# Attention loads reordered in a hybrid decoder layer: running sums and boundary values behind the first chunk's keys and queries

## The chip, the cores and the metric

The kernel runs on one core of a Trainium2 chip. The metric is the device time of one execution in microseconds (us), as the median of several runs; the profile is taken from one more execution on the same core, whose own time and span are given below. Engines are named as the profile names them: PE is TensorE's matmul side, PEld its weight loads, DVE is VectorE, ACT is ScalarE, POOL is GpSimd, SP is SyncE, which here issues nearly all transfers.

## The reference

One decoder layer over 2048 tokens of width 1024, in float32. The normed input is multiplied by `w_in`, and its columns go to four mixers: stick-breaking attention (A, 4 heads of 64), spatial gating (B), RWKV-7 time mixing (C) and forgetting attention (D, 4 heads of 64). The four results are concatenated, multiplied by `w_out` and added to the input; a mixture of 32 experts and a last norm follow. The change touches only the loads of A and D:

```python
# A: stick-breaking attention, per block of 128 queries
z = einsum('bhqd,bhkd->bhqk', q, k) * scale
log_one_minus = where(strict, log_sigmoid(-z), 0)
between = cumsum(log_one_minus, reverse=True) - log_one_minus
out = where(strict, exp(log_sigmoid(z) + between), 0) @ v
# D: forgetting attention
cum = cumsum(log_f)                       # one running sum per head
logits = q @ k.T * scale + cum[q] - cum[k]
out = softmax(where(causal, logits, -inf)) @ v
```

## The kernel before

The work is laid out in stages: `in_proj` (products with `w_in`, written to the DRAM scratch arrays `sT`, channels by tokens, and `sV`, tokens by channels), `rwkv`, `attention`, the output projection, routing, the experts. `forget_gate` writes the running sums of D to `cumD`. The program text runs `rwkv` to its end before `attention` starts, but the order in which each engine meets its instructions is set by a planner (`schedule_with_timeline_sim=True`): when the kernel is built, it goes through a simulated time line and gives each engine, at each moment, the earliest instruction of the text that is ready. So instructions of RWKV and of attention stand mixed in every engine's queue, and so do the transfers in SP's queue. On the chip each queue is then run strictly in the order written.

`attention` goes through the 4 heads of A (`sb` is true), then the 4 of D, each in 8 blocks of 256 queries. A head's keys, queries and values come in 4 chunks of 512 tokens; `Head.load(c)` brings chunk c when the first block that needs it starts. It loads the key rows twice into the two halves of a tile `raw` (L341), makes the rounded part `kh` (L344, ACT in A) and the rest `kl` (L345, POOL), loads the query rows in the same way into the other of the two `raw` buffers (L348), and makes `qs` (L350 on ACT, then L351 on POOL). Then come the values `v` (L353) and, in A, the values shifted by one token, `u` (L358 to L361), from which POOL makes differences (L362). In D a chunk of running sums, `nk`, comes instead (L365).

A block of A is: logits on PE (`logits`, L375, L376 and, on the diagonal, L378), `tanh` on ACT (L390), an affine step on POOL (L391), a running product on DVE (L393), transposes (L425), copies (L427) and products with `v` (L431). At the end of a block the boundary values `vc` (the last value row of each block of 128 tokens) are added: in block 0 by a DVE copy (L444), otherwise in an ACT instruction (L442). `vc` is loaded when a head of A is created (L335): 64 by 16 single elements of 4 bytes.

`cq` holds the running sums of D by query, [128, 16, 4]. Four transfers (L321), one per head, fill it at the top of `attention`, each of 2048 single elements of 4 bytes. It is read in `softmax` alone, by L408 and L409, in heads of D.

L667 loads the inputs of RWKV, L673 is the DVE instruction that consumes them, L157 writes the last blocks of `in_proj`, and L1027 to L1030 (`route_setup`) write initial tables for the routing; in the text they stand inside head 0 of A, ahead of everything of head 1.

Of the kernel before, what the change touches and what calls it, by code (L numbers as in the profile page):

```python
# [8 lines left out]
F32 = mybir.dt.float32  # L9
# [11 lines left out]
NT = 16  # L21
W = 256
NH = 4
HD = 64
# [4 lines left out]
def dram(ap, offset, pattern):  # L29
    return bass.AP(tensor=ap.tensor, offset=ap.offset + offset, ap=pattern)  # L30
# [277 lines left out]
def attention(tc, K, ctx, sT, sV, cumD, mixT):  # L308
    nc = tc.nc
    cp = ctx.enter_context(tc.tile_pool(name="at_c", reuse_waits="tile", bufs=1))  # L310
    hp = ctx.enter_context(tc.tile_pool(name="at_h", reuse_waits="tile", bufs=5))
    rp = ctx.enter_context(tc.tile_pool(name="at_r", reuse_waits="tile", bufs=2))
# [3 lines left out]
    ps = ctx.enter_context(tc.tile_pool(name="at_ps", reuse_waits="tile", bufs=4, space=PSUM))  # L316
    po = ctx.enter_context(tc.tile_pool(name="at_po", reuse_waits="tile", bufs=1, space=PSUM))
    cq = cp.tile([128, NT, NH], F32, name="cq")
    with nc.allow_non_contiguous_dma(reason="small"):
        for h in range(NH):  # L320
            nc.sync.dma_start(cq[:, :, h], cumD[h].rearrange("(i p) -> p i", p=128))  # L321

    def bank():
        return ps.tile([128, 512], F32, name="bk", tag="bk")
# [1 line left out]
    class Head:  # L326
        def __init__(self, h, sb):
            self.h, self.sb = h, sb
            self.q0, self.k0, self.v0 = (0, 256, 0) if sb else (512, 768, 256)
            self.q0, self.k0, self.v0 = (a + h * HD for a in (self.q0, self.k0, self.v0))  # L330
            self.kh, self.kl, self.qs, self.v, self.nk = [], [], [], [], []
            if sb:
                self.vc = cp.tile([64, NT], F32, name="vc", bufs=2)
                with nc.allow_non_contiguous_dma(reason="small"):
                    nc.sync.dma_start(self.vc, dram(sV, 127 * 516 + self.v0, [[1, HD], [128 * 516, NT]]))  # L335

        def load(self, c):
            h, t0 = self.h, c * 512
            raw = rp.tile([128, 512], F32, name="raw", tag="raw")
            for s in range(2):  # L340
                nc.sync.dma_start(raw[s * 64:s * 64 + 64], sT[self.k0:self.k0 + HD, t0:t0 + 512])  # L341
            kh = hp.tile([128, 512], F32R, name="kh")
            kl = hp.tile([128, 512], F32R, name="kl")
            (nc.scalar.activation(kh, raw, AF.Copy) if self.sb else nc.gpsimd.tensor_scalar(kh, raw, 1.0, 0.0, op0=OP.mult, op1=OP.add))  # L344
            nc.gpsimd.tensor_sub(kl, raw, kh.bitcast(F32))  # L345
            raw = rp.tile([128, 512], F32, name="raw", tag="raw")
            for s in range(2):
                nc.sync.dma_start(raw[s * 64:s * 64 + 64], sT[self.q0:self.q0 + HD, t0:t0 + 512])  # L348
            qs = hp.tile([128, 512], F32R, name="qs", bufs=2)
            (nc.scalar.activation(qs, raw, AF.Copy) if self.sb else nc.gpsimd.tensor_scalar(qs, raw, 1.0, 0.0, op0=OP.mult, op1=OP.add))  # L350
            nc.gpsimd.tensor_sub(qs[64:128], raw[64:128], qs[64:128].bitcast(F32))  # L351
            v = hp.tile([128, 4, HD], F32, name="v")
            nc.sync.dma_start(v, sV[t0:t0 + 512, self.v0:self.v0 + HD].rearrange("(i p) c -> p i c", p=128))  # L353
            if self.sb:
                u = rp.tile([128, 4, HD], F32, name="u")
                if c == 0:
                    nc.vector.memset(u[0:1, 0], 0.0)
                    nc.sync.dma_start(u[1:128, 0], sV[0:127, self.v0:self.v0 + HD])  # L358
                    nc.sync.dma_start(u[:, 1:4], sV[127:511, self.v0:self.v0 + HD].rearrange("(i p) c -> p i c", p=128))
                else:  # L360
                    nc.sync.dma_start(u, sV[t0 - 1:t0 + 511, self.v0:self.v0 + HD].rearrange("(i p) c -> p i c", p=128))  # L361
                nc.gpsimd.tensor_sub(v, u, v)  # L362
            else:
                nk = hp.tile([128, 512], F32, name="nk", bufs=4)
                nc.sync.dma_start(nk, cumD[h:h + 1, t0:t0 + 512].to_broadcast([128, 512]))  # L365
                nc.gpsimd.tensor_scalar(nk, nk, -8.0, 0.0, op0=OP.mult, op1=OP.add)
                self.nk.append(nk)
            for l, t in ((self.kh, kh), (self.kl, kl), (self.qs, qs), (self.v, v)):
                l.append(t)
# [1436 lines left out]
def model(ctx, tc, x, xT, g1, w_in, wsT, bT, mu, w0, w2, a0, a2, g2, k_k, k_a, r_k, gn_w, gn_b, bf, w_out, g2b,  # L1806
# [15 lines left out]
    with tc.tile_pool(name="r_consts", bufs=1) as rp:  # L1822
        R = RwConsts(tc, K, rp)
        rw = rwkv(tc, K, R, right, sT, prm, mixT)
        in_proj(tc, K, x, xT, g1, w_in, wsT, bT, bf, sT, sV, mixT, cumD, lambda j: [next(rw) for _ in range((0, 1, 2, 0)[j])])
        with ExitStack() as left:
            init = left.enter_context(tc.tile_pool(name="init", bufs=1))
            for _ in rw:
                pass
            mix = attention(tc, K, left, sT, sV, cumD, mixT)  # L1830
            for _ in range(60):
                next(mix)
            route_setup(tc, init, table, gtab, xacc)
            for _ in mix:
                pass
# [58 lines left out]
```

## Time and profile before

| | |
|---|---|
| median of 3 runs | 2596.97 us (2595.97 to 2601.28) |
| the profiled execution's own time | 2600.24 us |
| its span, first to last instruction | 2598.5 us |
| mean granted TensorE clock | 0.968 |
| busy share of the span: PE, DVE, ACT, POOL | 94%, 65%, 51%, 26% |

The span is the stretch that the trace covers; the execution's own time is 1.7 us longer. Busy shares are means over stages with different limits, so the stages have to be read one at a time: `in_proj` with the first part of RWKV up to about 597 us, attention with the rest of RWKV from there to about 1525 us, the output projection and the experts after that.

### The profile page before, as it was taken

Reading aid. Unit: us, or ns where it says so; the run is one execution under the profiler, and the core shown is the slowest. Engines: PE = TensorE matmul, PEld = TensorE weight load, DVE = VectorE, ACT = ScalarE, POOL = GpSimd, SP = SyncE. Lnnn points to the kernel's source line nnn. Section 1 sums busy time; section 2 is a strip of 40 time slices with the busy share of each in tenths; the row PEclk is TensorE's granted clock in tenths of the full one; section 3 lists DMA queues with packets and bytes.
Section 4 is the critical chain, followed back from the end, with each engine's and each line's share of the span. In section 5 each row is a group of like instructions: output and inputs, shape, how many; then the busy total and the mean of one; then the engine's idle time right before and its main releaser. Section 6 shows DMA issues by size and latency. Waiting matters only on the chain. (4 is left out here: it accounts for less than half of the span.)

```text
span 2598.5 us, 42227 instructions
## 1 busy us (share of the span) xinstructions
PE 2444.1 (94%) x14802; PEld 1753.0 (67%) x14803; DVE 1679.6 (65%) x3881; ACT 1322.4 (51%) x2527; POOL 677.1 (26%) x691
## 2 busy tenths in 40 slices
PE   8999999997989899999999999997999999999994
PEld 6789998874646464656556668874666676676663
DVE  5313402247797879786685756665777787787785
ACT  6201222224665564575566642222666776777774
POOL 2000000016364646331331022222212232222224
PEclk9999999998989998999999999998999999999997
DMA  8510222215121111111101056744979899899995
GB/s 258 163 63 26 80 69 67 71 60 124 35 53 29 47 39 39 47 50 47 49 27 48 10 171 180 234 139 114 339 263 352 309 320 368 292 324 356 328 316 169
DMA packets 241826, 394.73 MB, mean 152 GB/s; under 512 B 65921, under 2 KB 106753, under 8 KB 241608
## 3 DMA queue, kind: packets, MB, share of 16 engines
q1 hardware_dynamic: 222472, 336.68, 39.2%
q0 software_dynamic: 19136, 55.30, 7.6%
q8 instruction: 118, 1.93, 0.3%
q14 instruction: 100, 0.82, 0.1%
HBM read 319.24 MB, written 76.85 MB: 152 GB/s over the span
## 5 line engine op out<-in xcount | busy, mean ns | idle before, releaser
L72 DVE TENSOR_TENSOR wl<-wr,wh 128x1024 fp32r<-128x1024 f32 x366 | 442.4, 1222 | 116.9 <-ACT wh L71 106.8
L71 ACT ACTIVATE wh<-wr 128x1024 fp32r<-128x1024 f32 x366 | 381.4, 1057 | 150.7 <-PE pg L1456 57.9
L393 DVE TENSOR_TENSOR_SCAN S<-S,zero 128x512 f32<-128x512 f32 (+3 forms) x160 | 198.5, 1251 | 48.8 <-POOL S L391 48.6
L152 PE MATMUL p<-hhi,wh 128*128 128x512 f32 x512 | 205.5, 403 | 11.6 <-ACT hhi L112 6.5
L427 ACT ACTIVATE tq<-bk 128x512 f32<-128x512 f32 (+1 forms) x288 | 156.4, 571 | 103.6 <-PE bk L425 83.6
L425 PE MATMUL bk<-ident,S 128*128 128x128 f32 x1088 | 185.1, 291 | 25.0 <-DVE S L393 19.1
L153 PE MATMUL p<-hlo,wh 128*128 128x512 f32 x512 | 205.0, 400 | 0.0
L154 PE MATMUL p<-hhi,wl 128*128 128x512 f32 x512 | 204.5, 400 | 0.0
L431 PE MATMUL o<-tq,v 128*64 128x256 f32 (+1 forms) x1152 | 191.2, 403 | 4.5 <-ACT tq L427 2.6
L425 PEld LDWEIGHTS bk<-ident,S 128*128 128x128 f32 x1088 | 123.2, 144 | 100.7 <-issue 57.6
L156 DVE TENSOR_TENSOR e<-p,rb 128x512 f32<-128x512 f32 x64 | 43.6, 690 | 196.5 <-PE p L154 183.3
L391 POOL TENSOR_SCALAR S<-S 128x512 f32<-128x512 f32 (+3 forms) x160 | 125.6, 794 | 151.7 <-ACT S L390 136.5
L735 POOL TENSOR_TENSOR k<-big,k 128x512 f32<-128x512 f32 x8 | 14.2, 1772 | 550.6 <-DVE big L734 544.6
L375 PE MATMUL bk<-kh,qs 128*128 128x512 f32 (+2 forms) x320 | 148.1, 463 | 5.5 <-POOL qs L351 3.2
L171 PE MATMUL p<-wh,hhi 128*128 128x256 f32 (+1 forms) x512 | 144.5, 282 | 0.0
L172 PE MATMUL p<-wl,hhi 128*128 128x256 f32 (+1 forms) x512 | 144.4, 282 | 0.0
L173 PE MATMUL p<-wh,hlo 128*128 128x256 f32 (+1 forms) x512 | 143.7, 281 | 0.0
L152 PEld LDWEIGHTS p<-hhi,wh 128*128 128x128 f32 x512 | 97.6, 191 | 36.8 <-ACT hhi L112 6.2
L376 PE MATMUL bk<-kl,qs 128*128 128x512 f32 (+2 forms) x320 | 121.4, 381 | 0.0
L413 ACT ACTIVATE S<-S,bias 128x512 f32<-128x512 f32 (+3 forms) x160 | 103.6, 649 | 34.4 <-DVE bias L409 33.9
L71 ACT ACTIVATE wh<-raw 128x512 fp32r<-128x512 f32 (+1 forms) x52 | 27.7, 590 | 178.7 <-PE p L153 171.7
L1453 PE MATMUL pg<-wh,xh 128*128 128x512 f32 x248 | 102.6, 414 | 14.1 <-ACT s L1460 12.6
(559 smaller groups left out, 6153.5 us busy)
## 6 DMA issues: line engine op xcount, KB each, us to landing
wr<-in SPq DMA_DIRECT2D x386, 512.0 KB, 11.1
raw<-in SPq DMA_DIRECT2D x108, 256.0 KB, 4.1
sT<-e SPq DMA_DIRECT2D x64, 256.0 KB, 2.4
raw<-sT SPq DMA_DIRECT2D x128, 128.0 KB, 2.9
mr<-mixT SPq DMA_DIRECT2D x16, 512.0 KB
xt<-in SPq DMA_DIRECT2D x16, 512.0 KB
xacc<-xt SPq DMA_DIRECT2D x16, 512.0 KB, 4.8
h2D<-h SPq DMA_DIRECT2D x16, 512.0 KB, 8.6
```

What stands on the lines that cost most here:

```text
L71: nc.scalar.activation(hi, raw, AF.Copy)
L72: nc.vector.tensor_sub(lo, raw, hi.bitcast(F32))
L152: nc.tensor.matmul(p, wh[:, k, ms], hi[j][:, k], start=(k == 0), stop=False)
L153: nc.tensor.matmul(p, wh[:, k, ms], lo[j][:, k], start=False, stop=False)
L154: nc.tensor.matmul(p, wl[:, k, ms], hi[j][:, k], start=False, stop=(k == KD - 1))
L171: nc.tensor.matmul(p, a, wh[:, k], start=first and k == 0, stop=False, skip_group_check=True)
L172: nc.tensor.matmul(p, a, wl[:, k], start=False, stop=False, skip_group_check=True)
L375: nc.tensor.matmul(z[:, :w], q, self.kh[c][:, :w], start=True, stop=False)
L393: nc.vector.tensor_tensor_scan(r, r, K.zero.to_broadcast([128, w]), 1.0 if c == i // 4 else S[c + 1][:, 0:1], op0=OP.mult, op1=OP.add)
L425: nc.tensor.transpose(t[:, x:x + 128], S[a][j // 4][:, (j % 4) * 128:(j % 4) * 128 + 128], K.ident)
L427: nc.scalar.activation(tq[:, :w], t[:, :w], AF.Copy)
L431: nc.tensor.matmul(o[64 * e:64 * e + 64, o0:256], self.v[j // 4][:, j % 4], tq[:, x0:x1], start=first, stop=last, skip_group_check=True)
```

## The change

The four transfers into `cq` leave the top of `attention` and become a function, `sums()`. The load of `vc` leaves the head's constructor and becomes a method, `tails()`. Both are called at the end of the first chunk's load: `tails()` for every head of A, `sums()` once, in head 1 of A, behind that head's `tails()`. In `load`, the query rows are now asked for right behind the key rows; the arithmetic on both follows, in the order that it had. The instructions, their shapes, the number of transfers and the buffers are the same.

```diff
-    with nc.allow_non_contiguous_dma(reason="small"):
-        for h in range(NH):
-            nc.sync.dma_start(cq[:, :, h], cumD[h].rearrange("(i p) -> p i", p=128))
+
+    def sums():
+        with nc.allow_non_contiguous_dma(reason="small"):
+            for h in range(NH):
+                nc.sync.dma_start(cq[:, :, h], cumD[h].rearrange("(i p) -> p i", p=128))
...
-            if sb:
-                self.vc = cp.tile([64, NT], F32, name="vc", bufs=2)
-                with nc.allow_non_contiguous_dma(reason="small"):
-                    nc.sync.dma_start(self.vc, dram(sV, 127 * 516 + self.v0, [[1, HD], [128 * 516, NT]]))
+
+        def tails(self):
+            self.vc = cp.tile([64, NT], F32, name="vc", bufs=2)
+            with nc.allow_non_contiguous_dma(reason="small"):
+                nc.sync.dma_start(self.vc, dram(sV, 127 * 516 + self.v0, [[1, HD], [128 * 516, NT]]))
...
-            raw = rp.tile([128, 512], F32, name="raw", tag="raw")
-            for s in range(2):
-                nc.sync.dma_start(raw[s * 64:s * 64 + 64], sT[self.k0:self.k0 + HD, t0:t0 + 512])
+            raws = []
+            for r0 in (self.k0, self.q0):
+                raw = rp.tile([128, 512], F32, name="raw", tag="raw")
+                for s in range(2):
+                    nc.sync.dma_start(raw[s * 64:s * 64 + 64], sT[r0:r0 + HD, t0:t0 + 512])
+                raws.append(raw)
+            raw = raws[0]
...
-            raw = rp.tile([128, 512], F32, name="raw", tag="raw")
-            for s in range(2):
-                nc.sync.dma_start(raw[s * 64:s * 64 + 64], sT[self.q0:self.q0 + HD, t0:t0 + 512])
+            raw = raws[1]
...
                 nc.gpsimd.tensor_sub(v, u, v)
+                if c == 0:
+                    self.tails()
+                if c == 0 and h == 1:
+                    sums()
```

## Rows read from the trace of the kernel before

**Rows 1.** Busy time by stretch (instructions in brackets), granted clock, DMA share, GB/s

```profile
core 0: us, PE busy (x) PEld busy (x) DVE busy (x) ACT busy (x) POOL busy (x), PEclk, DMA share, GB/s
560.00:600.00 40.00, 37.89 (x201) 25.89 (x199) 21.91 (x63) 9.69 (x32) 5.06 (x16) 1.00 0.17 52
600.00:640.00 40.00, 28.22 (x204) 15.46 (x204) 32.04 (x49) 20.61 (x47) 32.16 (x30) 0.74 0.72 150
640.00:1520.00 880.00, 832.82 (x6171) 525.25 (x6167) 658.86 (x1651) 528.54 (x1348) 336.22 (x347) 0.96 0.16 41
720.00:760.00 40.00, 31.86 (x242) 19.34 (x242) 37.52 (x63) 19.43 (x42) 26.10 (x27) 0.85 0.29 65
1530.00:2590.00 1060.00, 994.00 (x5059) 709.01 (x5058) 777.39 (x1646) 615.22 (x834) 280.10 (x247) 0.97 0.82 277
```

**Rows 2.** Time line of SP's queue around the seam: start, duration, instruction

```profile
595.17 1.10 SPq L341 DMA_DIRECT2D raw<-sT  x2
596.38 0.52 SPq L157 DMA_DIRECT2D sT<-e  x1
596.95 5.85 SPq L321 DMA_DIRECT2D cq<-cumD  x4
602.84 1.74 SPq L335 DMA_DIRECT2D vc<-sV  x1
604.63 1.31 SPq L348 DMA_DIRECT2D raw<-sT  x2
...
609.48 1.09 SPq L341 DMA_DIRECT2D raw<-sT  x2
610.67 0.53 SPq L667 DMA_DIRECT2D raw<-sT  x1
...
611.78 1.10 SPq L348 DMA_DIRECT2D raw<-sT  x2
```

**Rows 3.** Time line of ACT at the seam; in brackets idle time before it

```profile
602.71 0.72 ACT L670 ACTIVATE big<-raw,om 128x512 f32<-128x512 f32 x1 [1.03 <-POOL k L735]
609.14 0.63 ACT L350 ACTIVATE qs<-raw 128x512 fp32r<-128x512 f32 x1 [5.70 <-DMA raw<-sT]
...
617.09 0.63 ACT L350 ACTIVATE qs<-raw 128x512 fp32r<-128x512 f32 x1 [2.58 <-DMA raw<-sT]
```

**Rows 4.** Time line of POOL at the seam

```profile
599.46 1.48 POOL L345 TENSOR_TENSOR kl<-raw,kh 128x512 fp32r<-128x512 f32 x1 [2.71 <-ACT kh L344]
...
603.92 1.31 POOL L743 TENSOR_TENSOR r<-r,k 128x512 f32<-128x512 f32 x1
609.90 1.27 POOL L351 TENSOR_TENSOR qs<-raw,qs 64x512 fp32r<-64x512 f32 x1 [4.67 <-ACT qs L350]
```

**Rows 5.** Time line of DVE at the seam

```profile
607.00 0.22 DVE L444 COPY ol<-vc 64x128 f32<-64x128 f32 x1 [2.88 <-DMA vc<-sV]
...
608.35 0.74 DVE L673 SCALAR_TENSOR_TENSOR lora<-raw,mu,big 128x512 f32<-128x512 f32 x1
...
611.45 1.61 DVE L673 SCALAR_TENSOR_TENSOR sg<-raw,mu,big 128x512 f32<-128x512 f32 x1 [0.75 <-ACT big L670]
...
619.64 1.21 DVE L393 TENSOR_TENSOR_SCAN S<-S,zero 128x256 f32<-128x256 f32 x1 [3.71 <-POOL S L391]
```

**Rows 6.** Time line of PE at the seam

```profile
605.28 2.08 PE L746 MATMUL bk<-r,rkb 128*128 128x512 f32 x2
610.05 0.66 PE L845 MATMUL bk<-xe,yv 128*32 128x128 f32 x8 [2.69 <-DVE yv L839]
611.22 0.47 PE L375 MATMUL bk<-kh,qs 128*128 128x128 f32 x1 [0.51 <-POOL qs L351]
...
619.17 0.47 PE L375 MATMUL bk<-kh,qs 128*128 128x128 f32 x1 [2.69 <-POOL qs L351]
```

**Rows 7.** Busy time of finer stretches at the seam; columns as in rows 1

```profile
596.00:602.00 6.00, 1.89 (x29) 0.95 (x28) 6.00 (x14) 1.26 (x2) 3.11 (x5) 1.00 0.61 90
602.00:614.00 12.00, 7.56 (x39) 3.70 (x39) 8.33 (x14) 3.81 (x7) 7.00 (x7) 0.50 0.63 88
...
626.00:640.00 14.00, 12.22 (x114) 7.55 (x113) 13.60 (x20) 11.22 (x28) 13.76 (x13) 1.00 0.59 134
```

**Rows 8.** Time line of SP's queue behind the seam

```profile
621.02 0.61 SPq L1027 DMA_DIRECT2D table<-tinit  x1
...
624.85 0.66 SPq L335 DMA_DIRECT2D vc<-sV  x1
...
630.50 1.45 SPq L359 DMA_DIRECT2D u<-sV  x1
```

**Rows 9.** The readers of the running sums: duration min/median/max in ns, first and last start

```profile
L408 DVE TENSOR_TENSOR bias<-m,cq x64: 107/154/1228, 1057.9 to 1508.3; 128x1 f32<-128x1 f32 x64
```

## The prediction

> **What bounds the kernel now.** I read the busy time by stretch first, then the time line of each queue where PE falls idle, then the same view in finer stretches.
>
> By stretch, PE is nearly full before the seam between `in_proj` and attention (37.89 of 40 us) and again behind it: 832.82 of 880 us from 640 to 1520 us, which leaves 47.2 us idle, and 994.00 of 1060 us in the last stage [rows 1]. Only the 40 us at the seam are far from full: PE 28.22, at a granted clock of 0.74 [rows 1]. So PE's work bounds the kernel nearly everywhere, and work that starts earlier at the seam should end earlier, unless the order behind it gets worse.
>
> SP's queue shows why the seam is slow. The first chunk's keys are asked for at 595.17; its queries stand behind the four transfers into `cq` (5.85 us) and `vc` (1.74 us) and are asked for at 604.63 [rows 2]. ACT, whose queue runs in order, stands 5.70 us until they land, and its `qs` starts at 609.14 [rows 3]. POOL stands 4.67 us behind it [rows 4], and the first logits start at 611.22 [rows 6]. Apart from that, DVE stands 2.88 us for `vc` at the copy of block 0 [rows 5], and all that follows in its queue, RWKV's work too, stands with it; PE's L845 then waits 2.69 us for DVE [rows 6]. The second chunk repeats the pattern: its queries leave SP at 611.78, ACT waits 2.58 us for them, PE 2.69 us, and DVE stands 3.71 us before its scan at 619.64 [rows 2, 3, 5, 6]. From 626 us on DVE (13.60 of 14 us) and POOL (13.76) are full [rows 7]. The seam's cost is therefore best counted as time that DVE stands idle before 619.64.
>
> **The change part by part.** *The queries of chunk 0.* With `cq` and `vc` gone from between, they follow L157 at about 596.95 instead of 604.63: 7.68 us earlier [rows 2]. From the end of their issue at 605.94 to `qs` on ACT were 3.20 us [rows 2, 3], so they land at about 596.95 + 1.31 + 3.20 = 601.5. Not all of the 7.68 us arrives. In the written order ACT has L670 until 603.43 [rows 3], POOL has L743 until 605.23 [rows 4], PE has L746 until 607.36 and then L845, which DVE releases [rows 6]. L845 comes 2.88 us earlier if DVE no longer waits for `vc`, at about 607.2. So the first logits start at about 608 instead of 611.22, some 3.3 us earlier; if the planner puts them ahead of RWKV's work they gain up to 7.7.
>
> *`vc` of head 0.* It is issued behind `v` and `u` of chunk 0, hence at about 600.5, and without the queue in front of it should take 0.66 us, as later [rows 8], against 1.74 [rows 2]. Its landing (607.00 less 604.58, the end of its issue, so 2.4 us) puts it at about 603.6; DVE gets to the copy at 607.00 - 2.88 = 604.1. The wait goes: 2.88 us of DVE [rows 5].
>
> *The second chunk.* Its keys need the buffer that `kl` releases at 600.94 [rows 4] and stand behind `vc`, so they can go at about 602 instead of 609.48 [rows 2]. Its queries are held by L667, which stands between them [rows 2]; L667 needs the buffer that L673 frees at 609.09 now and, without the 2.88 us, at 606.2 [rows 5]. With the 1.11 us from L667 to the queries (610.67 to 611.78) [rows 2] these go at about 607.3, 4.5 us earlier, and 4.5 us is what the written order gives. The transfer itself had a full load beside it, 4.21 us from issue to use (612.88 to 617.09) against 3.20 for chunk 0 [rows 2, 3], up to 1.0 us more to gain. So the scan at 619.64 starts 4.5 to 5.5 us earlier.
>
> The sum by DVE's idle time agrees: 2.88 us for `vc` and 0.75 us for L670, which stood in ACT's queue behind `qs`, go wholly, and of the 3.71 us the rest, 0.9 to 1.9 us [rows 5]. From below it is bounded by 2.9 us (the `vc` wait alone), from above by 7.7 us (all that SP gives back; DVE's three waits add up to 7.34) [rows 2, 5]. I take 6.0 us: the written order gives 5, and the planner can put attention's first instructions into the gaps of 4 to 6 us which ACT and POOL now show.
>
> The Trainium skill speaks against so large a price for the issues: by "DMA: Bandwidth & Descriptors", "Issuing engines are not separate DMA queues", the sequencer's time to start a transfer is usually small beside the transfer. The trace disagrees here: four transfers of 8 KB held SP for 5.85 us. With the 0.66 us that a later `vc` took [rows 8], five issues would be 3.3 us; the sum by the Trainium skill's rule would then be a gain of 3 us, 2594, which is the time of the second rival below and adds nothing to its chance.
>
> *`cq` at its new place.* It costs nothing where it is read, as L408 first reads it at 1057.9 [rows 9]. Its four issues will now stand in front of other loads. In the text they stand behind `u` of head 1's chunk 0, which went out at 630.50 [rows 8]. The tables of `route_setup` also need nothing that is late, and they stand in the text ahead of head 1; they went out at 621.02 only [rows 8]. So the planner has no free place for `cq` before that, and I expect it at 615 to 640. What it delays there are loads for blocks that come tens of us later, under a PE that is filling up: cost 0. Without that cover it is 5.85 us once.
>
> *`vc` of heads 1 to 3, and keys beside queries in later chunks.* The two `raw` buffers still alternate, so each load waits for the same instruction as before; no instruction is added and none lengthened: 0. If such a load came first, one issue of 0.66 us [rows 8].
>
> Nothing behind the seam waits for a fixed time, so the 6.0 us should arrive at the end: span 2598.5 - 6.0 = 2592.5, own time 2600.24 - 6.0 = 2594.2. The profiled execution is 3.3 us above the median of the runs; against that median the forecast is 2596.97 - 6.0 = **2591.0 us**.
>
> **Rivals.** *The clock stays up (faster).* PE's clock is at 0.50 from 602 to 614, after a stretch in which PE was busy 1.89 of 6 us [rows 7], and PE's 7.56 busy us there would be 3.8 at full clock. If the logits fill the gap soon enough, up to 3.8 us come on top, less what DVE hides; with 3 us the time is 2588. Against it: L845 of RWKV still waits on DVE [rows 6], and the idle stretch before 602 ends no earlier than the queries land, so a gap stays.
>
> *`cq` directly behind head 0's `vc` (no measurable change).* If the planner sees SP idle before chunk 1's keys, the 5.85 us move there, and chunk 1 goes out at about 608 against 609.48. Then only the 2.9 to 3.3 us of the first steps stay: 2594. The late tables speak against it.
>
> *The gain is swallowed.* RWKV or DVE sets a later stretch and attention's head start is spent waiting: 2597. For it speaks that DVE is full where PE is not (37.52 of 40 us from 720 to 760) [rows 1]; against it that RWKV's DVE work is released earlier too.
>
> *The planner deals the 900 us behind the seam differently, and worse (slower).* A shift of 5 us makes other instructions ready first. The place is a stretch like 720 to 760, where scans of attention meet RWKV's DVE work: PE loses 8.14 us there, at a clock of 0.85, which is 30% of 40 us at half speed, up to 6 us of work [rows 1]. One more such stretch costs 8 to 14 us against 6.0: 2599 to 2605, say 2603. It decides as soon as PE's idle time from 640 to 1520 grows from 47.2 by more than about 11 us. A fresh deal can as well shrink it.
>
> **How the numbers follow.** About 0.2% (5.2 us) can be told from no change. Chances: the forecast (2589 to 2594) 0.45, of which 0.37 beyond 5.2 us; the clock 0.12; `cq` ahead of chunk 1 0.20; swallowed 0.08; a worse deal 0.15. So faster 0.49, same 0.08 + 0.20 + 0.08 = 0.36, slower 0.15. The range reaches from the lower end of the clock case with a lucky deal, 2584, to 2602, which leaves out about half of the slower case and little else.
>
> **What the profile after would show.** Right: L348 of chunk 0 directly behind L341 or L157 near 597; no ACT wait of over 1 us at the first `qs`; no wait at L444; first logits near 604 to 608, the second chunk's near 614; `cq` behind the tables; PE's idle time from 640 to 1520 near 47 us, and all later landmarks 6 us earlier. Wrong: `cq` still ahead of chunk 1; L667 holding SP as long as before; or a seam that is shorter by 6 us and a stretch behind it that has lost as much.

## The result, and the profile after

The changed kernel is slower: 2611.07 us (median of 10 runs, 2606.97 to 2617.87) against 2594.68 us of the kernel before on the same chip (10 runs, 2587.49 to 2601.28), a ratio of 1.0069 with a 95% interval of 1.0057 to 1.0082 (the ratios here are estimates of their own, not quotients of the medians, so the two can differ by 1 to 3 us). The forecast was 2591.0, with 2602 as the upper end. The profiled execution took 2609.95 us, its span is 2608.3, and its mean granted clock 0.965 against 0.968. Lines stand further down than before: L321 (`cq`) is now L323, L335 (`vc`) L338, L344 L351, L350 L355, the loads L341 and L348 are both L346, and from L363 on it is 9 lines: L375 is L384, L444 L453, L667 L676.

At the seam the transfers came out nearly as forecast. SP's queue, from the time line, answers to [rows 2]:

```profile
595.88 1.09 SPq L346 DMA_DIRECT2D raw<-sT  x2
597.08 0.52 SPq L157 DMA_DIRECT2D sT<-e  x1
597.65 1.13 SPq L346 DMA_DIRECT2D raw<-sT  x2
...
602.76 0.64 SPq L338 DMA_DIRECT2D vc<-sV  x1
...
605.51 1.08 SPq L346 DMA_DIRECT2D raw<-sT  x2
607.93 0.34 SPq L676 DMA_DIRECT2D raw<-sT  x1
...
611.26 0.62 SPq L1036 DMA_DIRECT2D table<-tinit  x1
...
623.20 4.63 SPq L323 DMA_DIRECT2D cq<-cumD  x4
```

The queries of chunk 0 leave at 597.65 instead of 604.63, those of chunk 1 at 605.51 instead of 611.78 and no longer behind RWKV's load (L676), and `cq` goes out at 623.20, behind the tables. The other engines, each from its time line, answer to [rows 3, 5, 6]:

```profile
603.21 0.63 ACT L355 ACTIVATE qs<-raw 128x512 fp32r<-128x512 f32 x1 [2.89 <-DMA raw<-sT]
...
605.96 1.28 DVE L453 COPY ol<-vc 64x128 f32<-64x128 f32 x1
...
605.66 0.48 PE L384 MATMUL bk<-kh,qs 128*128 128x128 f32 x1
...
616.13 0.46 PE L384 MATMUL bk<-kh,qs 128*128 128x128 f32 x1
```

ACT's wait falls from 5.70 to 2.89 us, DVE's copy of `vc` waits for nothing, and the first logits start at 605.66 instead of 611.22, those of the second chunk at 616.13 instead of 619.17. By stretch (columns as in [rows 1], to which they answer):

```profile
600.00:640.00 40.00, 31.00 (x236) 18.64 (x237) 34.57 (x56) 23.35 (x57) 31.54 (x32) 0.77 0.79 159
640.00:1520.00 880.00, 827.22 (x6122) 523.42 (x6122) 652.89 (x1644) 524.47 (x1337) 323.83 (x345) 0.95 0.15 40
1530.00:2590.00 1060.00, 996.81 (x5062) 710.99 (x5062) 772.65 (x1624) 615.35 (x832) 274.93 (x243) 0.97 0.82 275
```

At the seam PE is busy 2.78 us more. Behind it, from 640 to 1520, its idle time is 52.8 us against 47.2. That is 5.6 us; the loss, 16.4 us by the medians, is three times as large, so idle time alone doesn't explain it. The finer view of the place where the two traces part shows the rest. The kernel before, then the changed one:

```profile
1090.00:1100.00 10.00, 10.00 (x63) 6.45 (x62) 9.29 (x39) 5.81 (x17) 2.37 (x3) 1.00 0.10 26
1100.00:1110.00 10.00, 9.31 (x61) 5.75 (x59) 8.56 (x30) 9.87 (x33) 3.81 (x3) 1.00 0.04 8
1110.00:1120.00 10.00, 10.00 (x75) 6.89 (x75) 7.99 (x28) 6.92 (x20) 0.00 (x0) 1.00 0.10 33
1120.00:1130.00 10.00, 8.65 (x82) 5.09 (x74) 8.95 (x37) 4.39 (x12) 1.92 (x2) 1.00 0.13 35
1130.00:1140.00 10.00, 8.84 (x58) 4.63 (x57) 10.00 (x19) 5.91 (x15) 8.37 (x7) 0.90 0.00 1
```

```profile
1090.00:1100.00 10.00, 7.63 (x35) 4.79 (x33) 9.66 (x29) 8.32 (x25) 3.76 (x3) 0.82 0.10 26
1100.00:1110.00 10.00, 9.88 (x37) 6.00 (x36) 2.96 (x10) 3.75 (x11) 0.00 (x0) 0.50 0.03 7
1110.00:1120.00 10.00, 10.00 (x70) 6.51 (x66) 7.23 (x28) 4.91 (x16) 0.00 (x0) 1.00 0.07 28
1120.00:1130.00 10.00, 9.78 (x83) 5.17 (x81) 8.71 (x32) 4.87 (x13) 1.34 (x2) 1.00 0.03 7
1130.00:1140.00 10.00, 6.93 (x36) 3.69 (x35) 9.50 (x28) 4.03 (x11) 8.90 (x8) 0.70 0.13 37
```

The column PEclk is the granted clock: 1.00 is the upper level of PE's clock (2.4 GHz), 0.50 the lower (1.2 GHz). Busy time times granted clock, summed over the five rows, is 45.9 us before and 35.8 after: 10 us of PE's work are missing in these 50 us, but only 2.6 us of busy time. From 1100 to 1110 PE looks full (9.88) and does half the work, at the lower level. PE's time line after shows what went ahead of it:

```profile
1092.84 0.28 PE L434 MATMUL bk<-ident,S 128*128 128x128 f32 x1
1095.19 0.30 PE L788 MATMUL bk<-ident,bkt 128*128 128x128 f32 x1 [2.07 <-DVE rkT L813]
...
1132.69 0.33 PE L841 MATMUL bk<-ident,xc 128*128 128x128 f32 x1 [1.53 <-DVE xc L856]
```

Each of the two half-clock stretches begins about 1 us behind such a wait. Both are waits of RWKV's instructions for DVE. In PE's queue many of RWKV's instructions stand 12 to 32 places further forward here than before, and attention's as far back, so attention's products stand behind waits that came later before, or not at all. That these waits bring the clock down is read from the order in time; no run takes one of them away alone.

### The profile page after: what moved, and what is told of

The parts are those of the page before. It is cut to its first block, busy times and chain, and to the rows that moved or that the text cites. A ratio compares the mean times of both kernels' runs of the same rounds, so it can differ in the third digit from the quotient of the medians.

```text
span 2608.3 us, 42233 instructions
## 1 busy us (share of the span) xinstructions
PE 2444.4 (94%) x14802; PEld 1756.3 (67%) x14803; DVE 1674.8 (64%) x3881; ACT 1323.0 (51%) x2527; POOL 661.5 (25%) x691
## 5 line engine op out<-in xcount | busy, mean ns | idle before, releaser
L434 PE MATMUL bk<-ident,S 128*128 128x128 f32 x1088 | 190.4, 295 | 29.6 <-DVE S L402 20.9
L400 POOL TENSOR_SCALAR S<-S 128x512 f32<-128x512 f32 (+3 forms) x160 | 115.0, 728 | 148.9 <-ACT S L399 141.6
L384 PE MATMUL bk<-kh,qs 128*128 128x512 f32 (+2 forms) x320 | 147.8, 462 | 3.0 <-DVE m L411 1.9
```

Of the source, the lines that this page charges most:

```text
L384: nc.tensor.matmul(z[:, :w], q, self.kh[c][:, :w], start=True, stop=False)
L434: nc.tensor.transpose(t[:, x:x + 128], S[a][j // 4][:, (j % 4) * 128:(j % 4) * 128 + 128], K.ident)
```

## Experiments

Two theories stood at first. *Order theory*: the planner dealt a new order, and that order is worse. *Load theory*: the moved transfers delay something where they now stand; narrowed later to the *delay theory*, that `cq`'s four transfers hold up whatever loads follow them closely. To part them, the order of PE, DVE, ACT and POOL is written out and imposed: a table of each queue's order, and at the end of the program a dependency without a semaphore from each instruction to the next of its queue.

```python
def follow(tc):
    ...
    tc.add_manual_dep(l[k], last.name, mybir.DependencyInfo(mybir.DependencyClass.NoSync, ...), reason="order")
```

The change turns 3143 of PE's 12114 places, 1105 of DVE's 3718, 741 of ACT's 2270 and 141 of POOL's 762. Moving `cq` and `vc` does all of it: with the pairing of keys and queries alone, every queue comes out as it was, so that part was not run.

**keep_order** (the first replay). The kernel before with its own order imposed; only SP's queue is edited.

```diff
 SP's queue
-  cq x4, vc of head 0            (in front of the queries of chunk 0)
   queries, v, u of chunk 0
+  vc of head 0
 ...
   u of head 1's chunk 0
+  cq x4
```

> Every engine's queue is written in the order that it had before the change; only in SP's queue the four loads of cq and head 0's vc stand at the places that the change gives them. Order theory (the loads help, the planner's new order behind the seam costs): the gain at the seam arrives, 4 to 8 us below the kernel before, so about 2587 to 2591, the first logits near 608. Load theory (the loads at their new place delay something behind the seam): as slow as the changed kernel, 10 to 18 us above the kernel before.

**new_order_old_loads.** The mirror image: the changed kernel's order everywhere, `cq` and `vc` back in front of the first queries.

```diff
 SP's queue
   keys of chunk 0
+  cq x4, vc of head 0
   queries, v, u of chunk 0
-  vc of head 0
 ...
-  cq x4
```

> The mirror image: every engine's queue in the order of the changed kernel, but cq and head 0's vc back in front of the first queries in SP's queue. Order theory: it keeps the loss and also loses the gain at the seam, 15 to 25 us above the kernel before. Load theory: about the time of the kernel before, within 5 us.

keep_order: 2596.08 us (before 2596.14), ratio 0.9999 [0.9987, 1.0012]. new_order_old_loads: 2614.37, ratio 1.0066 [1.0046, 1.0087]. The loss goes with the order, whole, wherever the two loads stand, as order theory had it (15 to 25 us for the second kernel; it is 18). But keep_order fits neither theory: it is not faster, though its seam is shorter: the scan at 619.64 [rows 5] starts at 616.81. Its trace says where that went. SP, ACT, and by stretch:

```profile
631.00 4.69 SPq L321 DMA_DIRECT2D cq<-cumD  x4
...
639.44 0.59 SPq L341 DMA_DIRECT2D raw<-sT  x1
...
645.85 0.63 ACT L344 ACTIVATE kh<-raw 128x512 fp32r<-128x512 f32 x1 [4.88 <-DMA raw<-sT]
```

```profile
633.00:635.00 2.00, 0.87 (x10) 0.52 (x8) 2.00 (x2) 1.91 (x6) 2.00 (x2) 1.00 0.57 4
635.00:637.00 2.00, 1.88 (x15) 1.26 (x15) 1.97 (x5) 0.68 (x2) 2.00 (x2) 1.00 0.96 7
641.00:643.00 2.00, 1.84 (x14) 1.14 (x13) 0.00 (x0) 0.00 (x0) 0.00 (x0) 1.00 1.06 254
643.00:645.00 2.00, 0.00 (x0) 0.00 (x0) 0.00 (x0) 0.00 (x0) 0.96 (x2) 1.00 0.94 211
```

Behind `cq`, keys asked for at 639.44 are waited for until 645.85, and at 643 to 645 PE, DVE and ACT all stand. The DMA engines are 0.96 busy at 7 GB/s while the elements of `cq` go through (635 to 637); behind them come the whole loads that stood in the queue, at 254 and 211 GB/s (641 to 645), so the keys wait in line with these too. The Trainium skill, "DMA: Bandwidth & Descriptors", "Why small descriptors are slow (HBM only)", says that each piece carries a fixed overhead, which weighs the more the smaller the piece; the trace agrees (7 GB/s with single elements, 254 with whole loads, at a like busy share).

The changed kernel has the same wait behind its own `cq`, on ACT and, by stretch, on PE, which stands from 637 to 639:

```profile
636.73 0.63 ACT L351 ACTIVATE kh<-raw 128x512 fp32r<-128x512 f32 x1 [2.60 <-DMA raw<-sT]
```

```profile
637.00:639.00 2.00, 0.00 (x0) 0.00 (x0) 1.97 (x3) 1.84 (x5) 1.56 (x1) 1.00 0.61 192
```

**cq_only, vc_only.** One half of the change each, dealt afresh by the planner.

```diff
 cq_only                                  vc_only
-    cq[:, :, h] <- cumD (top)           -    self.vc <- sV (constructor)
+    if c == 0 and h == 1: sums()        +    if c == 0: self.tails()
```

> cq alone is moved, vc stays in the constructor, the planner orders everything anew. Order theory: another deal, whose time may lie on either side; the seam gains 3 to 6 us (5.85 us of SP), the stretch behind it anything from -10 to +20 us. Load theory: with most of the moved transfers it shows most of the loss, +8 to +16 us.

> vc alone is moved, cq stays at the top. Order theory: another deal; the seam gains about 1 to 3 us (1.74 us of SP, the wait of DVE for vc stays in part), behind it anything from -10 to +20 us. Load theory: without cq at its new place hardly a loss, within 4 us of the kernel before.

cq_only: 2608.17, 1.0046 [1.0032, 1.0060]. vc_only: 2601.39, 1.0018 [1.0002, 1.0034]. Each half alone brings another order, and neither is faster; as the deals differ, the two don't add up to anything that could be read. They don't part the theories: cq_only, 12 us slower, lies in both ranges, and vc_only, 5 us slower, lies 1 us outside load theory's 4. In cq_only the clock is at 1.00 from 1090 to 1150; its trace loses most in the output projection, where PE is busy 109.33 us at a clock of 0.90 from 1520 to 1640, against 112.66 at 0.97 in the kernel before. So a worse deal can lose in another place.

**cq_late, after_cq_late.** `cq` alone moved on in SP's queue, to where SP and the DMA engines stand idle (behind a store at 798.8 us of the kernel before); all other queues as in keep_order and as in the changed kernel.

```diff
 SP's queue
-  cq x4            (631.00 in keep_order, 623.20 in the changed kernel)
 ...
   mixT<-oo         (798.82 before)
+  cq x4
```

> The order of the kernel before on PE, DVE, ACT and POOL, as in the first replay, with head 0's vc behind u of its first chunk; but the four transfers into cq stand in SP's queue behind the store that went out at 798.8 in the kernel before, where SP then stood idle for 14.6 us. In the first replay they stood at 631.0 to 635.7, and ACT then stood 4.88 us for keys behind them. If cq's transfers hold up whatever load follows them (delay theory), the wait of ACT near 646 goes back to nothing, the landmarks from 650 to 790 stand 3 to 4 us ahead of the kernel before instead of 3.5 us behind it, and the end comes 2 to 5 us earlier, near 2592, if nothing behind absorbs it. If gains of a few us are absorbed anyway (absorption theory), the landmarks near 650 are ahead but the time stays within 2595 to 2598. If cq at 631 cost nothing, the landmarks don't change against the first replay.

> The order of the changed kernel on every engine, with cq's four transfers alone put behind the same store near 797 in SP's queue. By the delay theory the wait of ACT for keys near 636 (2.60 us) and the full stop of PE from 637 to 639 go, and the time falls by 2 to 5 us against the changed kernel, to 2606 to 2609. By the order theory the loss of 11 to 15 us between 1095 and 1240 stays, since RWKV's products keep standing 12 to 30 places further ahead in PE's queue there; so the time stays above 2601 in any case. If the late loads alone made the loss, 2596 or less.

**cut_1095, cut_cq_late.** By 1095 us both orders have dealt the same instructions on each queue, so one can be continued by the other: the changed kernel's order up to there, the old one behind; the second one with `cq` late as well.

```diff
 each queue, from about 1095 us on
-  the changed kernel's order
+  the order of the kernel before
```

> The changed kernel's order on all queues up to about 1095 us, and the order of the kernel before from there on (the same instructions have been dealt on each queue by then, so the two halves fit). Its cq stays at 623. Order theory, with the loss in the stretch from 1095 to 1240: PE stands 6 us ahead at 1095, as in the changed kernel, and stays ahead; 11 to 16 us of the loss go, and the time is 2594 to 2599. If the loss there comes from the time at which the work arrives and not from its order (the clock falling by chance, or work that is ahead having to wait), the half-clock stretch near 1097 stays and the time stays at 2607 to 2614.

> As the one with the changed kernel's order up to 1095 and the old one behind, and with cq's transfers near 797 as well. If delay theory and order theory both hold, their gains add up: 2 to 5 us below that kernel, 2589 to 2596, which would be a version at or below both kernels. If the order behind 1095 isn't the cause, 2604 to 2611.

**cut_reverse, cut_1300.** The same the other way round (old order and old loads to 1095, new order behind), and the changed kernel's order up to about 1385 us, which leaves only the start of the output projection to the old one.

> The order of the kernel before on all queues up to about 1095 us, cq and vc in front of the first queries as there, and the changed kernel's order from 1095 on. Order theory: the seam and everything to 1095 are as before, then the stretch from 1095 to 1240 and the output projection lose what they lose in the changed kernel, 11 to 18 us, so 2605 to 2612. If the changed kernel's order behind 1095 is only bad for work that arrives 6 us early, or the clock fell there by chance, 2594 to 2599.

> The changed kernel's order up to about 1385 us, the order of the kernel before from there on; the two differ behind 1385 only in the start of the output projection (1536 to 1615) and a few places near the end. It splits the loss behind 1095: if the stretch from 1095 to 1300 carries nearly all of it, 2607 to 2611; if the output projection's order carries a part, as PE's idle time of 7.7 us from 1530 to 1640 against 3.8 and the half clock behind it suggest, that part of 4 to 6 us goes and the time is 2604 to 2607.

| kernel | order before 1095 / 1095 to 1300 / behind | `cq` at, us | median us | ratio [95%] |
|---|---|---|---|---|
| changed | new / new / new | 623 | 2611.07 | 1.0069 [1.0057, 1.0082] |
| after_cq_late | new / new / new | 791 | 2608.85 | 1.0048 [1.0029, 1.0066] |
| cut_1300 | new / new / old | 624 | 2608.64 | 1.0041 [1.0027, 1.0055] |
| cut_reverse | old / new / new | 597 | 2613.11 | 1.0063 [1.0047, 1.0079] |
| cut_1095 | new / old / old | 626 | 2595.11 | 0.9996 [0.9981, 1.0011] |
| keep_order | old / old / old | 631 | 2596.08 | 0.9999 [0.9987, 1.0012] |
| cut_cq_late | new / old / old | 790 | 2589.69 | 0.9984 [0.9970, 0.9998] |
| cq_late | old / old / old | 796 | 2589.12 | 0.9985 [0.9970, 1.0000] |

The kernel before had medians of 2594.55 to 2596.52 beside them. The last six kernels to be run, those with `late` or `cut` in their names, came in the ranges that delay and order theory gave them, but for cut_reverse (1.1 us above its range) and cq_late (5.4 us down by the medians where 2 to 5 were expected). The new order behind 1095 makes the loss whether the work arrives early or at its old time (changed, cut_reverse), and without it the loss is gone (cut_1095). From 1.0041 to 0.9996 lies the stretch from 1095 to 1300, some 12 us. From 1.0069 to 1.0041 lies the start of the output projection, some 7 us by the ratios and 4 by the medians. This second part is not shown as well: cut_1300 came in the range that was given for the case that the first stretch carries nearly all (2607 to 2611), the two intervals nearly touch, and the 4 us that its trace saves there (rows 1595.2 and 1640.1 of the list below) are gone again at 1829.8. In the same view as above, cut_1095 has the clock at 1.00 throughout:

```profile
1090.00:1100.00 10.00, 9.52 (x56) 6.18 (x55) 8.18 (x29) 4.55 (x16) 4.05 (x4) 1.00 0.13 33
1100.00:1110.00 10.00, 9.21 (x52) 5.32 (x52) 8.55 (x31) 9.43 (x29) 2.15 (x2) 1.00 0.00 0
1130.00:1140.00 10.00, 8.83 (x66) 4.21 (x66) 10.00 (x21) 6.13 (x16) 8.39 (x8) 1.00 0.09 22
```

The half clock from 1095 to 1110 came in the profile of every kernel with the new order there (five of five) and in none with the old one (five of five, the kernel before among them). So it is no accident of one execution.

With `cq` late, ACT's wait behind it is gone; the row of cq_late that answers to 645.85 above:

```profile
640.30 0.62 ACT L344 ACTIVATE kh<-raw 128x512 fp32r<-128x512 f32 x1
```

In after_cq_late the stop of PE from 637 to 639 is gone too (2.00 us busy of 2); smaller waits of ACT for queries and keys stay, 0.67 and 1.51 us. In its own new place `cq` meets nothing: PE is busy 15.00 of 15 us from 796 to 811. The delay theory holds in three pairs that differ in nothing else (keep_order and cq_late, changed and after_cq_late, cut_1095 and cut_cq_late): by 5.4, 2.1 and 5.4 us in the medians, each taken against the kernel before beside it (3.6, 5.4 and 3.1 by the ratios; one pair alone would be at the edge of what can be told), and by 4.5 to 7.2 us at 735.1 in the traces below, less what they differ by at 590.1. These are starts of the same PE instruction, at the same place of the queue in all these kernels (in the row 633.5 a few places apart), less its start in the kernel before:

```
before   changed after_cq_late cut_1300 cut_reverse cut_1095 cut_cq_late keep_order cq_late
 590.1    +0.7       +0.7        +0.7      -0.3       +2.5      -0.1        +0.7      +0.6
 633.5    -4.7       -6.0        -6.0      +2.5       -2.2      -6.8        -1.3      -1.8
 735.1    -1.4       -7.0        -0.2      +1.7       -1.9      -9.0        +3.5      -3.8
1054.2    -6.0       -8.6        -4.9      -4.0       -3.1     -13.3        -2.5      -9.9
1242.9    +4.2       +2.4        +8.4      +7.3       -2.6     -12.9        -3.2     -10.8
1500.0    +1.9       +3.7        +5.2      +3.8      -10.8     -19.3       -11.4     -18.9
1595.2    +2.4       +4.7        +4.6      +4.2      -11.9     -20.0        -9.7     -17.2
1640.1    +6.2      +10.7        +4.4      +6.5       -8.7     -20.5       -10.1     -17.5
1829.8    +6.0      +10.4       +10.1      +8.4       -1.8     -11.6        -3.4     -11.2
2400.0    +6.6       +7.8        +8.5      +8.4       -1.6     -13.5        -0.5     -11.3
```

From 633.5 to 735.1 the changed kernel gives back 3.3 us and keep_order 4.8, cut_1300 5.8 but cut_1095 only 0.3, and the kernels with a late `cq` give back nothing. From 1054.2 to 1242.9 all four kernels with the new order lose 10 to 13 us. Single profiles vary by several us (the kernel before's own is 5.7 us above its median beside cq_late), so the last rows are no measure of the times. Up to 1095 cut_reverse has the order and the loads of the kernel before and still stands +2.5 to -4.0 from it: what a column shares with cut_reverse there is the profile of the kernel before and not the change.

cq_late and cut_cq_late are the fastest: 5.4 and 4.9 us under the kernel before beside them by the medians, 3.9 and 4.2 by the ratios. Their intervals end at 1.0000 and 0.9998, so this gain is just at the edge of what can be told.

## Why the prediction was wrong

*Queries and first logits: right.* Queries at 597.65 (forecast 596.95, and this profile runs 0.7 us late from the start), first logits at 605.66 (forecast 604 to 608), no wait at `vc`. ACT still waits 2.89 us for the first `qs`; "no wait of over 1 us" was wrong, since the planner moved `qs` ahead of other ACT work.

*The second chunk and `vc`: less than forecast.* The second chunk's logits came at 616.13 (forecast 614): 3.0 us earlier by the clock of the trace, 3.7 without the 0.7. The `vc` term, 2.88 us that "goes" whole, starts from a wrong number. `vc` is put "at about 600.5", but from the queries' issue to the end of `u` SP needs 4.75 us in the kernel before (604.63 to 609.38, below), so by its own rows it goes out at 601.7, and it went out at 602.76. The changed kernel shows no wait, but DVE comes to the copy later there, at 605.96. In the written order, which the prediction reckoned with and keep_order runs, a part of the wait stays. SP before, then DVE in keep_order:

```profile
607.02 2.36 SPq L359 DMA_DIRECT2D u<-sV  x1
```

```profile
605.43 0.56 DVE L444 COPY ol<-vc 64x128 f32<-64x128 f32 x1 [0.64 <-DMA vc<-sV]
616.81 1.21 DVE L393 TENSOR_TENSOR_SCAN S<-S,zero 128x256 f32<-128x256 f32 x1 [3.33 <-POOL S L391]
```

In cq_late the copy waits 2.34 us for `vc` (issued at 603.17), and the scan starts at 616.20. So the scan came 2.8 and 3.4 us earlier, 3.5 and 4.0 without the late start, where 4.5 to 5.5 was forecast.

*The sum of 6.0 us: fits at the end, not at the seam.* With the old order behind it and `cq` out of the way the kernel gains 5.4 us by the medians of cq_late (3.9 by the ratio, whose interval goes from 0 to 7.8). At the seam the same kernel gains no more than the 4 us above. That the end agrees is therefore in part luck, and where the rest arises is not shown.

*"`cq` at its new place ... costs nothing": wrong.* The place was forecast well (615 to 640; 623.20), its price was not. What stood behind it were keys that were wanted at once, not loads for blocks tens of us later. The cover named, loads that come late enough, wasn't there, and the price without it had been given as 5.85 us once; it measured 4.5 to 7.2 us in the traces and 2.1 to 5.4 in the medians. This alone takes the forecast to no change (keep_order, 0.9999).

*"Nothing behind the seam waits for a fixed time, so the 6.0 us should arrive at the end": the step that turned the sign.* No instruction waits for a fixed time, but the order in which the queues were dealt does depend on when things become ready: PE's differs from 605 to 1298 us and again from 1536 to 1615. The new order behind 1095 costs some 16 us (2613.11 with the old loads in cut_reverse, against 2596.52; without it, cut_1095 takes 2595.11). The rival of a worse deal had been named, with 0.15. Its mechanism was right, its place and its test were not: the loss isn't another stretch like 720 to 760 (31.32 us busy against 31.86 in [rows 1]) but 1095 to 1140 and, less surely, the start of the output projection; and it "decides" with 5.6 us of added idle time, not above 11, because the test counted idle time and most of the loss from 1090 to 1140 is busy time at half clock (2.6 of 10 us are idle). Its size, 8 to 14 us for one such stretch, fits the 12 us from 1095 to 1300; a second place was not foreseen.

*The clock stays up:* it did a little at the seam (0.77 against 0.74), which decided nothing.

*The Trainium skill's rule on issue time* ("DMA: Bandwidth & Descriptors", "Issuing engines are not separate DMA queues") was set against 5.85 us for `cq`'s four issues; they took 4.63 to 6.25 us in the new places. In the changed kernel one issue takes 1.29 us (median) of the 3.2 us from issue to landing, so here it isn't small beside the transfer.

Open: which of the moved instructions between 1095 and 1300 starts the stall (with the old order on one engine alone and the new one on the others, the queues could wait for each other, so that wasn't tried), and why a head start of 17 to 20 us at 1640 is 11 to 12 at 1830.

## What to carry to other kernels

A load that is moved has a price where it lands: look at which load stands right behind the new place and when it is wanted, and put transfers of many single elements where the queue and the DMA engines are idle for longer than they take. Where a planner deals the queues, an edit that shifts the work by a few us can change the order far behind it, and that can cost more than the edit brings; pin the old order to measure the edit itself, and price a new order in PE's busy time times its clock, not in idle time.

## What the runs showed of the hardware

A short wait could be dear through the clock. In the changed kernel PE ran at 1.2 GHz from 1096 to 1110 behind a wait of 2.07 us, which costs about 7 us of work, more than three times the wait; the next, of 1.53 us, was followed by some 7 us at half clock. Not every such wait is: in keep_order a wait of 1.35 us, which ends at 1124.85, left the clock at 1.00, and in new_order_old_loads waits of 0.95, 0.20 and 0.59 us between 1095 and 1098 were followed by half clock. The length of one wait alone doesn't decide. A busy share near full hides this: the rows from 1100 to 1110 differ by 0.57 us in the wrong direction.

In keep_order four transfers of 8 KB in single elements of 4 bytes kept the DMA engines 0.96 busy at 7 GB/s from 635 to 637, and a load of 128 KB that was issued 3.8 us behind the last of them was waited for until 5.8 us after its issue had ended. Other loads, at 211 to 254 GB/s, lay between; with `cq` elsewhere (cq_late) ACT had no wait there.
